# A new issue order for the first part of a one-core trunk layer, with tiles of the modulation moved from VectorE to TensorE

## The chip, the core and the metric

The kernel runs on one core of one Trainium2 chip. The metric is the device time of one execution in microseconds, from a median over runs; lower is better. The core has a matrix engine (TensorE, PE in the profile), a vector engine (VectorE, DVE), an activation engine (ScalarE, ACT), a general engine (GpSimd, POOL) and a queue engine that issues most of the DMAs (SyncE, SP). Each engine works through its own instructions in order and waits on semaphores for the others.

## What is computed

One layer of a diffusion trunk on 1024 tokens of width 1024. Cut to what matters here (the pooling mixer is the one that layer 0 uses):

```
mod_x = silu(c) @ mod_w + mod_b                  # 1024 -> 6 * 1024
sh1, sc1, g1, sh2, sc2, g2 = split(mod_x, 6)
hx  = x * (1 + sc1) + sh1
ox  = multiscale_pool(hx, pool_w, pool_scale)    # 4 groups of 256 channels, windows 2, 4, 8, 16
x   = layer_norm(ALPHA * x + g1 * ox, ln_g[0], ln_b[0])
h   = x * (1 + sc2) + sh2
gt, up = split(h @ ffn_w_in, 2)                  # 1024 -> 2 * 2816
x   = layer_norm(ALPHA * x + g2 * ((silu(gt) * up) @ ffn_w_out), ln_g[1], ln_b[1])
```

Inputs and outputs are float32. `mod_w` alone is 24 MB: each of its six parts (`SH1`, `SC1`, `G1`, `SH2`, `SC2`, `G2`) comes as eight tiles of 128 x 1024.

## The kernel before

Tokens lie in two halves of four blocks of 128 rows: `ORDER = ((1, 2, 3, 4), (5, 6, 7, 0))`. A matrix product in float32 is made of three passes of a rounded format (`mm3`): each operand is split into a high part (`take_hi`, ScalarE) and the rest (`take_lo`, VectorE), and TensorE adds high x high, high x low and low x high.

The kernel has three parts. The **first part** holds the modulation, the pooling, the first norm and the gate product of half 0. Each step of it is a job with a name and a number, and the table `ORDER_OF_ISSUE` lists all jobs in the order in which they are issued. The table therefore sets the order on every engine at once. A second table, `PLACE_OF`, says which PSUM bank (eight of them) and which SBUF buffer (45 large ones) each tile takes; a tile waits until the tile before it in that place has been read for the last time. The **second part** runs 22 periods (`period`) of the products of the feed-forward layer for both halves, with banks `ps_v`. The **third part** makes the output product (`sub_pass`, banks `ps_x` and `ps_y`) and the second norm. The second and the third part are issued by loops that the change doesn't touch.

Jobs of the first part that matter below, by engine:

- SP: `mod_load` (one tile of `mod_w`, named `mw_j_k` for part j and tile k; part 1 is `SC1`, 2 `G1`, 3 `SH2`, 4 `SC2`, 0 `SH1`), `load_x`, `mod_start` (loads a bias row into an accumulator that GpSimd has cleared), `gate_load`, `gate_out`, `keep_row`.
- TensorE: `pool_inner` and `pool_outer` (the window means of a column tile `ct` of half 0 or 1, into bank `ps_pt`), `pooled` (12 matmuls, bank `ps_ox`: the pool weights on four tiles of the means), `mod_col` (8 matmuls, bank `ps_col`: turns a summed modulation row into columns), `mod_whole` (8 matmuls: the same straight from one tile of `mod_w` and the column of silu(c)), `g1_bank`, `turned` (four transposes of x, bank `ps_h`), `gate_step` (6 matmuls of the gate product, bank `ps_gate`; 88 steps, two to eight of each pair of columns at a time).
- VectorE: `mod_add` (adds one tile of `mod_w`, scaled, to the accumulator), `pool_lo`, `make_g1`, `pool_w_weigh`, `pool_w_lo`, `residual` (empties a bank `ps_ox` into x), `mean`, `factor`, `mod_col_done`, `finish_gain`, `finish_shift`, `gate_lo`, `hidden_lo`, and for half 1 `difference` and `t_lo`.
- ScalarE: `pool_hi`, `pool_w_hi`, `start_band`, `end_band`, `spread`, `norm`, `scaled_h` (empties `ps_h` with gain and shift), `hidden_hi`, `gate_hi`, `gate_first`, `gate_done`, `t_hi`.

`mod_columns(j, by_tensor)` shares out the eight tiles of one part: tiles in `by_tensor` become `mod_whole`, the others `mod_add`, and a last `mod_col` adds the accumulator into the same bank. For `SH2` the kernel before gives tiles 0 and 1 to TensorE, for `SC2` none:

```
order = [k for k in range(KT) if k not in by_tensor]
for k in range(KT):
    if k in by_tensor:
        job(mod_whole, j, k, k == by_tensor[0], k == by_tensor[-1] and not order)
    else:
        job(mod_add, j, k, k == order[0])
if order:
    job(mod_col, j, not by_tensor)
```

The last chain before the gate product: all `mod_add` of `SC2` and `SH2`, `mod_col` of both, `finish_gain`, `finish_shift`; and beside it `pooled` and `residual` of half 0, `mean`, `spread`, `factor`, `norm`; then `turned`, `scaled_h`, `hidden_hi`, `hidden_lo`, and `gate_step.0`.

Of the kernel before, what the change touches and what calls it, by code (L numbers as in the profile page):

```python
# [48 lines left out]
mod_load.11 mod_add.4 mod_load.12 mod_load.13 mod_load.14 pool_inner.11 pool_inner.3 mod_load.15 pool_inner.15
pool_inner.7 load_pool_w.0 load_pool_w.1 mod_add.5 load_x.4 pool_outer.2 load_x.5 pool_outer.0 pool_hi.2 pool_outer.3  # L50
pool_outer.1 load_x.6 pool_hi.0 pool_inner.24 pool_lo.2 pool_inner.16 load_x.7 pool_inner.25 pool_hi.3 pool_inner.17
mod_load.16 mod_add.6 pool_inner.28 pool_hi.1 pool_inner.20 mod_load.17 pool_inner.26 pool_inner.18 pool_inner.29
mod_load.18 pool_lo.0 pool_inner.21 start_band.0 scale_bank.0 mod_add.7 mod_load.19 end_band.0 scale_bank.1
scale_row.0 mod_add.8 mod_load.20 mod_col.0 scale_row.1 mod_add.9 mod_load.21 pool_inner.27 pool_outer.6
mod_col_done.0 pool_lo.3 pool_inner.19 pool_outer.4 pool_hi.6 pool_inner.30 mod_add.10 mod_load.22 pool_hi.4
pool_inner.22 pool_inner.31 pool_outer.7 pool_inner.23 pool_outer.5 pool_hi.7 mod_add.11 mod_load.23 pool_hi.5
mod_add.12 mod_load.24 mod_add.13 mod_load.25 mod_add.14 mod_load.26 mod_add.15 mod_load.27 g1_bank.0 pool_lo.1
pool_lo.6 pool_lo.4 g1_bank.1 pool_lo.7 pool_lo.5 make_g1.0 make_g1.1 pool_inner.40 pool_inner.32 pool_w_weigh.0
pool_inner.44 pool_w_weigh.1 pool_inner.36 pool_inner.41 pool_w_weigh.2 pool_inner.33 pool_w_weigh.3 pool_inner.56
pool_inner.48 pool_w_weigh.4 pool_inner.45 pool_w_hi.0 pool_inner.37 pool_w_weigh.5 pool_inner.42 pool_w_weigh.6  # L60
pool_inner.34 pool_inner.57 pool_w_lo.0 pool_inner.49 pool_inner.46 pool_inner.38 pool_inner.43 pool_outer.10 pooled.0
pool_w_weigh.7 pool_hi.10 mod_add.16 mod_load.28 pool_w_hi.1 pooled.2 residual.0 mod_add.17 mod_load.29 pooled.4
mod_add.18 mod_load.30 pool_inner.35 pool_outer.8 pool_inner.47 pool_hi.8 pool_outer.11 residual.2 pool_inner.39
pool_outer.9 pool_hi.11 pool_inner.59 mod_add.19 mod_load.31 gate_load.0 gate_load.1 gate_load.2 gate_load.3
gate_load.4 gate_load.5 pooled.6 pool_hi.9 mod_add.20 pool_outer.14 pool_inner.51 pool_outer.12 pool_inner.58
mod_add.21 pool_inner.50 pool_hi.14 pool_hi.12 residual.4 residual.6 pool_inner.60 mod_add.22 pool_inner.61
pool_inner.52 pool_inner.53 mod_add.23 pool_inner.63 pool_outer.15 pool_inner.55 pool_w_lo.1 pool_outer.13
pool_inner.62 pool_inner.54 pool_lo.10 pool_hi.15 mod_add.24 pool_hi.13 mod_whole.0 pool_lo.8 mod_add.25 mod_whole.1
mod_add.26 pooled.1 mod_add.27 residual.1 pooled.3 mod_add.28 mod_add.29 residual.3 mod_col.2 gate_hi.0 mean.0
spread.0 mean.1 gate_lo.0 pooled.5 spread.1 pool_lo.11 pooled.7 factor.0 residual.5 factor.1 norm.0 mod_col.1 mean.2  # L70
residual.7 keep_row.0 spread.2 mean.3 pool_lo.9 spread.3 pool_lo.14 pooled.12 factor.2 finish_gain.0 finish_shift.0
pooled.14 factor.3 norm.1 pool_lo.12 keep_row.1 norm.2 pool_lo.15 pooled.8 norm.3 pool_lo.13 keep_row.2 pooled.13
residual.12 keep_row.3 gate_hi.2 residual.14 turned.0 gate_hi.1 turned.1 residual.13 gate_lo.2 turned.2 scaled_h.0
turned.3 turned.4 scaled_h.1 gate_lo.1 turned.5 hidden_hi.0 turned.6 turned.7 pooled.15 residual.8 scaled_h.2
scaled_h.3 hidden_lo.0 hidden_hi.1 pooled.10 residual.15 scaled_h.4 hidden_lo.1 gate_step.0 scaled_h.5 hidden_hi.2
gate_step.1 residual.10 scaled_h.6 hidden_lo.2 scaled_h.7 gate_step.2 hidden_hi.3 gate_step.3 gate_hi.4 hidden_lo.3
gate_hi.3 gate_step.4 gate_lo.4 gate_hi.5 gate_lo.3 gate_step.5 gate_lo.5 gate_step.6 mod_load.32 gate_first.0
gate_step.7 mod_load.36 mod_add.30 gate_out.0 gate_first.1 gate_step.8 mod_load.33 gate_out.1 gate_step.9 mod_load.34
gate_step.10 mod_load.35 gate_step.11 gate_load.6 gate_load.7 gate_step.12 mod_add.31 gate_done.0 gate_out.2
gate_step.13 gate_step.14 mod_add.32 gate_step.15 load_pool_w.2 load_pool_w.3 mod_add.33 gate_first.2 gate_step.16  # L80
mod_load.37 mod_add.34 gate_out.3 gate_hi.6 gate_step.17 mod_load.38 gate_lo.6 gate_hi.7 gate_step.18 mod_load.39
gate_lo.7 gate_step.19 gate_load.8 gate_load.9 gate_step.20 gate_done.1 gate_out.4 gate_step.21 gate_step.22
mod_add.35 gate_step.23 gate_first.3 gate_step.24 gate_out.5 gate_step.25 mod_add.36 gate_step.26 mod_add.37
# [1325 lines left out]
```

## Time and profile before

| | |
|---|---|
| median of 3 runs | 749.86 us (748.98 to 750.0) |
| the profiled execution, its own time | 749.97 us |
| its span, first to last instruction | 748.2 us |
| PE busy | 723.9 us (97%) |
| DVE, ACT, POOL busy | 554.9, 274.1, 168.3 us |
| mean granted TensorE clock | 0.967 of full |

The span is cut into stretches by time. PE busy is the time in which at least one matmul is under way; the granted clock says how fast those matmuls ran (1.00 is 2.4 GHz, 0.50 is 1.2 GHz). A stretch in which PE is busy all the time at 1.00 can't get shorter by a change of order; a stretch with idle time or at 0.50 can. The gate product begins at 95.28 us and PE reaches the periods some 130 us later.

### The profile page before, as it was taken

How to read it: one execution, taken by the hardware profiler on the slowest of the kernel's cores; microseconds unless marked ns; L12 is line 12 of the kernel's file. 1: busy time of each engine (PE TensorE's matmuls, PEld its weight loads, DVE VectorE, ACT ScalarE, POOL GpSimd, SP SyncE). 2: the span in 40 equal slices, each digit the busy share in tenths (PEclk: the TensorE clock that was granted, in tenths of full speed). 3: DMA queues.
4: the chain of work that ended last, by engine and by line, in shares of the span. 5: the costliest groups of instructions: out<-in, count | busy, mean ns of one | idle time of the engine just before them, and what ended most of it. 6: DMA issues, size and time to landing. Idle time of an engine off the chain costs nothing.

```text
span 748.2 us, 9131 instructions
## 1 busy us (share of the span) xinstructions
PE 723.9 (97%) x3326; PEld 604.8 (81%) x3326; DVE 554.9 (74%) x675; ACT 274.1 (37%) x353; POOL 168.3 (22%) x133
## 2 busy tenths in 40 slices
PE   6988999999999999999999999999999999999994
PEld 6768988888887888888888888888888888888783
DVE  3797855517288788899998777965878679646986
ACT  0321873435983221311312212212556334336411
POOL 0000000011206546483743624600000000233100
PEclk7587999999999999999999999999999999999998
DMA  8998249674929679797987798455799856999612
GB/s 303 368 409 298 114 159 375 225 237 164 330 86 292 200 239 254 210 310 241 320 264 186 240 265 212 156 202 207 277 376 391 290 193 220 262 302 286 173 57 84
DMA packets 115346, 182.85 MB, mean 244 GB/s; under 512 B 7739, under 2 KB 66819, under 8 KB 115046
## 3 DMA queue, kind: packets, MB, share of 16 engines
q1 hardware_dynamic: 108038, 164.97, 63.8%
q0 software_dynamic: 7264, 17.30, 11.5%
q8 instruction: 26, 0.43, 0.2%
q14 instruction: 18, 0.15, 0.1%
HBM read 142.14 MB, written 51.64 MB: 259 GB/s over the span
## 4 chain that ended last, share of the span: by engine, by line
PE 84%; DVE 7%; DMA 3%; ACT 3%; issue 2%; POOL 0%; SPq 0%; POOLq 0%; DVEq 0%; ACTq 0%
PE ps_v L895 39%; PE ps_x L1106 16%; PE ps_gate L761 14%; PE ps_y L1106 8%; PE ps_col L506 2%; DVE acc L491 2%; DVE ylo L270 1%; PE ps_ox L262 1%; PE ps_ox L263 1%; PE ps_ox L264 1%; DMA x<-in_x 1%; DMA consts<-in_consts 1%; ACT h L699 1%; DMA mw<-in_mod_w 1%; DVE t L270 1%
## 5 line engine op out<-in xcount | busy, mean ns | idle before, releaser
L895 PE MATMUL ps_v<-t,w0h 128*128 128x512 f32 x352 | 109.2, 391 | 0.0
L761 PE MATMUL ps_gate<-h,wih 128*128 128x512 f32 x352 | 109.0, 391 | 0.0
L267 ACT CAST yhi<-yraw 128x1024 fp32r<-128x1024 f32 x77 | 78.4, 1051 | 81.7 <-DMA yraw<-in_ffn_w_out 23.4
L270 DVE TENSOR_TENSOR ylo<-yraw,yhi 128x1024 fp32r<-128x1024 f32 x77 | 91.6, 1218 | 20.6 <-ACT yhi L267 11.4
L962 POOL TENSOR_TENSOR s<-raw,raw 128x512 f32<-128x512 f32 x22 | 31.5, 1432 | 319.3 <-DMA raw<-in_ffn_w_in 300.5
L918 ACT ACTIVATE a<-a 128x512 f32<-128x512 f32 x22 | 13.9, 632 | 229.9 <-DVE a L917 229.9
L895 PEld LDWEIGHTS ps_v<-t,w0h 128*128 128x128 f32 x352 | 66.1, 188 | 14.6 <-issue 1.0
L761 PEld LDWEIGHTS ps_gate<-h,wih 128*128 128x128 f32 x352 | 65.7, 188 | 13.7 <-issue 0.5
L491 DVE SCALAR_TENSOR_TENSOR acc<-mw,s_col,acc 128x1024 f32<-128x1024 f32 x42 | 55.9, 1331 | 19.1 <-DMA mw<-in_mod_w 18.3
L895 PE MATMUL ps_v<-t,w0l 128*128 128x512 f32 x176 | 68.6, 390 | 1.4 <-DVE w0l L270 1.4
L761 PE MATMUL ps_gate<-h,wil 128*128 128x512 f32 x176 | 68.5, 389 | 0.0
L1106 PE MATMUL ps_x<-yhi 128*128 128x512 f32 x176 | 68.5, 389 | 0.0
L1106 PE MATMUL ps_x<-ylo,yhi 128*128 128x512 f32 x176 | 68.5, 389 | 0.0
L1106 PE MATMUL ps_x<-yhi,ylo 128*128 128x512 f32 x176 | 68.5, 389 | 0.0
L895 PE MATMUL ps_v<-t,ws 128*128 128x512 f32 x264 | 63.4, 389 | 0.0
L1068 POOL DMA_DIRECT2D yraw<-in_ffn_w_out x22 | 18.7, 853 | 195.6 <-PE ps_x L1106 163.6
L895 PEld LDWEIGHTS ps_v<-t,ws 128*128 128x128 f32 x264 | 49.5, 188 | 10.3
L895 PE MATMUL ps_v<-h,w1h 128*128 128x512 f32 x176 | 54.2, 389 | 0.0
L895 PE MATMUL ps_v<-t,w1h 128*128 128x512 f32 x176 | 54.2, 389 | 0.0
L1106 PE MATMUL ps_y<-yhi 128*128 128x512 f32 x132 | 51.4, 390 | 0.9 <-DVE yv L1352 0.9
L1106 PE MATMUL ps_y<-yhi,ylo 128*128 128x512 f32 x132 | 51.4, 389 | 0.0
L1106 PE MATMUL ps_y<-ylo,yhi 128*128 128x512 f32 x132 | 51.4, 389 | 0.0
(157 smaller groups left out, 1386.5 us busy)
## 6 DMA issues: line engine op xcount, KB each, us to landing
mw<-in_mod_w SPq DMA_DIRECT2D x48, 512.0 KB, 9.2
raw<-in_ffn_w_in SPq DMA_DIRECT2D x88, 256.0 KB, 5.2
wi<-in_ffn_w_in SPq DMA_DIRECT2D x22, 512.0 KB, 6.2
yraw<-in_ffn_w_out SPq DMA_DIRECT2D x44, 256.0 KB, 5.4
yraw<-ed SPq DMA_DIRECT2D x33, 256.0 KB, 6.0
ed<-in_ffn_w_out POOLq DMA_DIRECT2D x6, 1024.0 KB, 10.5
pd<-pk SPq DMA_DIRECT2D x11, 512.0 KB, 5.2
gd<-gk SPq DMA_DIRECT2D x11, 512.0 KB, 2.9
```

Of the source, the lines that this page charges most:

```text
L262: nc.tensor.matmul(ps, lh, rh, start=first, stop=False)
L263: nc.tensor.matmul(ps, lh, rl, start=False, stop=False)
L267: nc.scalar.copy(hi, src)
L270: nc.vector.tensor_tensor(lo, src, hi.bitcast(F32), ALU.subtract)
L491: nc.vector.scalar_tensor_tensor(acc, w, s_col[:, k : k + 1], acc, ALU.mult, ALU.add)
L506: nc.tensor.matmul(tiles["ps_col", j][:, n * WIDE : (n + 1) * WIDE], t[:, n * P : (n + 1) * P], by, start=first and n == 0, stop=last and ...
L761: nc.tensor.matmul(ps, x, y, start=k == n == 0, stop=k % 4 == 3 and n == 2, skip_group_check=k > 3)
L895: nc.tensor.matmul(ps, x, y, start=fresh and first, stop=last, skip_group_check=not fresh)
L918: nc.scalar.activation(a[:, 1], a[:, 1], ACT.Silu)
L962: nc.gpsimd.tensor_tensor(s, up1, up2, ALU.add)
L1068: nc.gpsimd.dma_start(raw[n][:, 1], ADDED[n // PAIRS](n % PAIRS), accum_op=ALU.add)
L1106: nc.tensor.matmul(ps, s[x][:, r * P : (r + 1) * P], t[y][:, d], start=fresh and j == m == 0, stop=j == PAIRS - 1 and m == 2, skip_group_c ...
```

## The change

The change writes the table `ORDER_OF_ISSUE` anew, with the table of places that belongs to it, and changes which tiles of the second modulation go to TensorE: tile 0 of `SC2` (before: none), and tiles 0 and 7 of `SH2` (before: 0 and 1). No job is added or taken away but for these: `mod_whole` three times in place of two, `mod_add` 37 times in place of 38. The second and third part, all shapes and all arithmetic stay.

```
-BY_TENSOR = (0, 1)
+BY_TENSOR = (0, 7)
...
-vector_rows.0 fill_constants.0 fill_ones.0 mod_load.0 mod_start.0 warm_up.0 load_consts.0 mod_load.1 load_x.0
+vector_rows.0 fill_constants.0 fill_ones.0 mod_start.0 warm_up.0 mod_load.0 load_consts.0 mod_load.1 load_x.0
...
-ps_warm ps_pt0_4 ps_pt1_1 ps_ox1_3_0 ps_h0_5 ps_gate2_0 ps_gate5_1 ps_ox1_1_1 ps_gate9_0
+ps_warm ps_pt0_6 ps_pt1_2 ps_pt1_5 ps_ox1_2_1 ps_gate3_1 ps_h1_4 ps_h1_1 ps_gate7_1
...
-    mod_columns(SC2, ())
+    mod_columns(SC2, (0,))
```

In the table of banks six of the eight `pooled` results of half 0 now share one bank, one after the other: `ps_ox0_0_0 ps_ox0_0_1 ps_ox0_3_0 ps_ox0_2_0 ps_ox0_1_0 ps_ox0_1_1`. On SP the first `mod_start` now stands ahead of the first `mod_load`. The order of all other loads up to the gate weights is as it was. On PE `mod_col` of `SH1` and the two `shift_bank` that follow from it now stand after gate steps 24 and 27, where they stood after steps 26 and 56, and the eight `turned` of half 1 after steps 39 to 41, where they stood after step 71. Four `pooled` of half 1 follow gate step 8, where two followed step 56.

VectorE, `G1` of the modulation (part 2, `acc2`) and the columns of `SC1` (`sc1`). Before, from the last tile of `SC1` on:

```order
L491 SCALAR_TENSOR_TENSOR acc1_192<-mw_1_7_229,s_col_71,acc1_192 128x1024
L491 SCALAR_TENSOR_TENSOR acc2_158<-mw_2_0_233,s_col_71,acc2_158 128x1024
L491 SCALAR_TENSOR_TENSOR acc2_158<-mw_2_1_236,s_col_71,acc2_158 128x1024
L518 SCALAR_TENSOR_TENSOR sc1_73<-ps_col1_323,cols_67 128x8
L474 TENSOR_TENSOR pt0_11_279<-ps_pt0_3_210,pt0_01_269 128x512
L491 SCALAR_TENSOR_TENSOR acc2_158<-mw_2_2_239,s_col_71,acc2_158 128x1024
L491 SCALAR_TENSOR_TENSOR acc2_158<-mw_2_3_243,s_col_71,acc2_158 128x1024
```

The same place in the changed kernel:

```order
L490 SCALAR_TENSOR_TENSOR acc1_188<-mw_1_7_228,s_col_71,acc1_188 128x1024
L490 SCALAR_TENSOR_TENSOR acc2_156<-mw_2_0_233,s_col_71,acc2_156 128x1024
L473 TENSOR_TENSOR pt0_12_332<-ps_pt0_4_301,pt0_02_330 128x512
L490 SCALAR_TENSOR_TENSOR acc2_156<-mw_2_1_236,s_col_71,acc2_156 128x1024
L490 SCALAR_TENSOR_TENSOR acc2_156<-mw_2_2_239,s_col_71,acc2_156 128x1024
L490 SCALAR_TENSOR_TENSOR acc2_156<-mw_2_3_242,s_col_71,acc2_156 128x1024
L490 SCALAR_TENSOR_TENSOR acc2_156<-mw_2_4_246,s_col_71,acc2_156 128x1024
L490 SCALAR_TENSOR_TENSOR acc2_156<-mw_2_5_248,s_col_71,acc2_156 128x1024
L490 SCALAR_TENSOR_TENSOR acc2_156<-mw_2_6_250,s_col_71,acc2_156 128x1024
L490 SCALAR_TENSOR_TENSOR acc2_156<-mw_2_7_254,s_col_71,acc2_156 128x1024
L473 TENSOR_TENSOR pt0_12_332<-ps_pt0_5_351,pt0_02_330 128x512
L517 SCALAR_TENSOR_TENSOR sc1_73<-ps_col1_321,cols_67 128x8
```

The step that reads the columns of `SC1` from TensorE's bank (`sc1`) stood among the adds of `G1` and now stands behind all of them.

TensorE, where two tiles of `SH2` (`mw_3_*`) go through `mod_whole` into bank `ps_col3`. Before, with the last window means of half 1 (`ps_pt1`) ahead and `pooled` of half 0 behind:

```order
L461 MATMUL ps_pt1_7_533<-starts_306,x0_283 128x128
L466 MATMUL ps_pt1_7_533<-consts_72,halo_207 128x2x8
L461 MATMUL ps_pt1_5_537<-starts_306,x0_283 128x128
L466 MATMUL ps_pt1_5_537<-consts_72,halo_207 128x2x8
L461 MATMUL ps_pt1_7_533<-ends_314,x7_273 128x135
L461 MATMUL ps_pt1_5_537<-ends_314,x7_273 128x131
L506 MATMUL ps_col3_555<-s_col_71,mw_3_0_361 128x64 x8
L506 MATMUL ps_col3_555<-s_col_71,mw_3_1_364 128x64 x8
```

The same two in the changed kernel, behind the last `pooled` of half 0 (`ps_ox0_3_1`), with window means of half 1, the `mod_col` of `SH2` and the first transpose behind:

```order
L263 MATMUL ps_ox0_3_1_611<-wpsh1_421,pt0_13_378 128x256
L505 MATMUL ps_col3_630<-s_col_71,mw_3_0_349 128x64 x8
L505 MATMUL ps_col3_630<-s_col_71,mw_3_7_480 128x64 x8
L460 MATMUL ps_pt1_4_657<-consts_72,x5_263 128x132
L460 MATMUL ps_pt1_4_657<-consts_72,x6_269 128x135
L460 MATMUL ps_pt1_4_657<-starts_266,x0_280 128x128
L465 MATMUL ps_pt1_4_657<-consts_72,halo_207 128x2x8
L460 MATMUL ps_pt1_4_657<-ends_276,x7_273 128x131
L505 MATMUL ps_col3_630<-ones_69,acc3_555 128x64 x8
L460 MATMUL ps_pt1_5_689<-consts_72,x5_263 128x132
L460 MATMUL ps_pt1_5_689<-consts_72,x6_269 128x135
L693 MATMUL ps_h0_2_692<-ident_68,x1_177 128x128
```

`mod_whole` of `SH2` moved from the middle of the window means and `pooled` of half 0 to behind all `pooled` of half 0, directly ahead of the transposes.

VectorE, at the end of the gate product, where the split weights of the second part begin (`w1l`, `ws1`, `w0l` of block 0, 1). Before:

```order
L270 TENSOR_TENSOR w1l_0_1890<-raw0_1_1337,w1h_0_1888 128x1024
L854 TENSOR_TENSOR h32_1_3_1716<-h32_1_3_1716,h32_0_1_831 128x1024
L270 TENSOR_TENSOR ws1_1_1905<-s1_1883,ws1_1_1905 128x512
L854 TENSOR_TENSOR h32_0_3_877<-h32_0_3_877,h32_1_3_1716 128x1024
L270 TENSOR_TENSOR t2_11_1867<-h32_1_3_1716,t2_01_1863 128x1024
L270 TENSOR_TENSOR t4_11_1869<-h32_0_3_877,t4_01_1865 128x1024
L270 TENSOR_TENSOR w0l_1_1910<-raw1_0_1553,w0h_1_1908 128x1024
```

The same place in the changed kernel:

```order
L269 TENSOR_TENSOR wil10_0_1763<-wi_10_0_1718,wih10_0_1740 128x1024
L269 TENSOR_TENSOR wil10_1_1774<-wi_10_1_1720,wih10_1_1765 128x1024
L269 TENSOR_TENSOR w1l_0_1897<-raw0_1_1485,w1h_0_1895 128x1024
L269 TENSOR_TENSOR ws1_1_1912<-s1_1890,ws1_1_1912 128x512
L269 TENSOR_TENSOR w0l_1_1917<-raw1_0_1678,w0h_1_1915 128x1024
```

The differences and splits of half 1 (`h32`, `t2`, `t4`) that stood between the weights of the second part have moved far ahead, into the middle of the gate product.

## Rows read from the trace of the kernel before

**Rows 1.** The page, busy time of TensorE: busy microseconds, share of the span, instructions.

```profile
PE 723.9 (97%) x3326; PEld 604.8 (81%) x3326; DVE 554.9 (74%) x675; ACT 274.1 (37%) x353; POOL 168.3 (22%) x133
```

**Rows 2.** Stretches of the span: from:to and length, then the busy time of PE, PEld, DVE, ACT and POOL (instructions), the granted clock, the DMA share and GB/s.

```profile
20.60:40.20 19.60, 16.75 (x68) 14.14 (x68) 14.94 (x16) 6.81 (x14) 0.00 (x0) 0.59 1.01 379
40.20:61.60 21.40, 21.13 (x132) 17.56 (x132) 20.55 (x33) 5.67 (x9) 0.00 (x0) 0.93 1.03 408
61.60:78.40 16.80, 14.41 (x73) 14.09 (x73) 11.97 (x17) 3.22 (x6) 0.00 (x0) 0.59 0.61 200
78.40:95.30 16.90, 16.90 (x147) 16.90 (x147) 13.63 (x34) 16.73 (x23) 0.00 (x0) 1.00 0.41 152
95.30:225.00 129.70, 129.70 (x607) 107.95 (x606) 67.05 (x93) 78.26 (x108) 10.33 (x8) 1.00 0.65 225
240.00:700.00 460.00, 460.00 (x2027) 380.14 (x2026) 369.26 (x409) 147.75 (x174) 145.43 (x109) 1.00 0.82 255
```

**Rows 3.** Waits of TensorE over the whole span: who was waited for, us in total, times, longest.

```profile
PE ps_g L548 <- DVE acc L491: 2.9, 1, 2.9
PE ps_col L506 <- DVE pt L474: 1.6, 1, 1.6
PE ps_v L895 <- DVE w0l L270: 1.4, 1, 1.4
```

**Rows 4.** TensorE in order of time, before the gate product: start, length, line, what, count, and the idle time ahead of it where there was some. A float32 matmul of the code shows as two, so eight columns of `mod_col` or `mod_whole` are x16.

```profile
40.23 3.51 PE L548 MATMUL ps_g<-acc,ones 128*128 128x512 f32 x4 [2.89 <-DVE acc L491]
43.58 2.41 PE L461 MATMUL ps_pt<-consts,x 128*128 128x130 f32 x20
...
63.23 6.56 PE L506 MATMUL ps_col<-s_col,mw 128*128 128x64 f32 x32 [1.60 <-DVE pt L474]
...
73.25 0.58 PE L262 MATMUL ps_ox<-wpsh,pt 128*128 128x256 f32 x1 [0.79 <-DVE x L608]
...
75.97 2.63 PE L506 MATMUL ps_col<-ones,acc 128*128 128x64 f32 x16
...
81.36 1.90 PE L506 MATMUL ps_col<-ones,acc 128*128 128x64 f32 x16
...
88.91 3.65 PE L694 MATMUL ps_h<-ident,x 128*128 128x128 f32 x32
92.33 0.36 PE L262 MATMUL ps_ox<-wpsh,pt 128*128 128x256 f32 x1
...
95.28 0.63 PE L761 MATMUL ps_gate<-h,wih 128*128 128x512 f32 x2
...
95.98 0.62 PE L761 MATMUL ps_gate<-h,wih 128*128 128x512 f32 x2
```

**Rows 5.** VectorE in order of time over the same stretch, columns as in rows 4.

```profile
31.53 0.17 DVE L518 SCALAR_TENSOR_TENSOR sc<-ps_col,cols 128x8 f32<-128x8 f32 x1 [3.01 <-PE ps_col L506]
...
32.21 7.88 DVE L491 SCALAR_TENSOR_TENSOR acc<-mw,s_col,acc 128x1024 f32<-128x1024 f32 x6
40.01 3.07 DVE L474 TENSOR_TENSOR pt<-ps_pt,pt 128x512 fp32r<-128x512 f32 x5
...
44.39 2.85 DVE L570 SCALAR_TENSOR_TENSOR wp<-wp,sc,g 128x256 f32<-128x256 f32 x7
...
48.70 0.75 DVE L489 TENSOR_SCALAR acc<-mw,s_col 128x1024 f32<-128x1024 f32 x1
...
61.36 1.22 DVE L270 TENSOR_TENSOR wpsl<-wp,wpsh 128x1024 fp32r<-128x1024 f32 x1
...
72.50 0.69 DVE L608 SCALAR_TENSOR_TENSOR x<-x,ps_ox 128x512 f32<-128x512 f32 x1 [4.22 <-PE ps_ox L264]
...
73.11 2.60 DVE L491 SCALAR_TENSOR_TENSOR acc<-mw,s_col,acc 128x1024 f32<-128x1024 f32 x2
```

**Rows 6.** ScalarE in order of time, the norms and the hidden tiles of half 0.

```profile
85.40 3.50 ACT L645 ACTIVATE x<-x,mv 128x1024 f32<-128x1024 f32 x3
...
90.68 1.44 ACT L699 ACTIVATE h<-ps_h,shift,gain 128x512 f32<-128x512 f32 x2
92.16 1.05 ACT L267 CAST h<-h 128x1024 fp32r<-128x1024 f32 x1
```

**Rows 7.** ScalarE, then VectorE, in order of time where the second part begins.

```profile
231.79 0.62 ACT L267 CAST ws<-s 128x512 fp32r<-128x512 f32 x1 [3.02 <-POOL s L962]
232.32 1.05 ACT L267 CAST t<-h 128x1024 fp32r<-128x1024 f32 x1
...
233.40 2.18 DVE L270 TENSOR_TENSOR t<-h,t 128x1024 fp32r<-128x1024 f32 x1 [2.88 <-ACT t L267]
235.50 2.30 DVE L270 TENSOR_TENSOR w0l<-raw,w0h 128x1024 fp32r<-128x1024 f32 x1
```

**Rows 8.** SP's queue at the start: start and length of the issue of a DMA.

```profile
1.20 0.36 SPq L295 DMA_DIRECT2D mw<-in_mod_w  x1
2.27 0.25 SPq L383 DMA_DIRECT2D acc<-in_mod_b  x1
```

**Rows 9.** SP, VectorE and TensorE around the last tile of `SH1`, in the gate product.

```profile
118.31 0.86 SPq L295 DMA_DIRECT2D mw<-in_mod_w  x2
...
127.48 2.61 DVE L491 SCALAR_TENSOR_TENSOR acc<-mw,s_col,acc 128x1024 f32<-128x1024 f32 x2 [1.22 <-DMA mw<-in_mod_w]
...
133.39 1.89 PE L506 MATMUL ps_col<-ones,acc 128*128 128x64 f32 x16
```

More of the change, by code (lines that the diff above doesn't have):

```diff
@@ L49 @@
[L49 to L83, printed above, removed]
@@ new lines @@
+mod_whole.0 mod_load.28 pool_w_lo.1 pooled.0 mod_add.16 mod_load.29 mod_add.17 mod_load.30 pool_outer.8 pool_inner.63
+pool_outer.15 pool_inner.61 residual.0 pool_inner.43 pool_outer.10 pool_inner.34 pooled.1 mod_add.18 mod_load.31
+gate_load.0 gate_load.1 gate_load.2 gate_load.3 gate_load.4 gate_load.5 pool_hi.10 pool_hi.8 mod_add.19 pool_inner.47
+pool_outer.11 pool_inner.38 pool_hi.11 pool_inner.62 pool_inner.58 residual.1 pool_hi.9 mean.0 pooled.6 mod_add.20
+pool_hi.14 spread.0 mod_add.21 residual.6 mod_add.22 pooled.4 pool_hi.15 factor.0 mod_col.1 mod_add.23 norm.0
@@ new lines @@
+residual.4 keep_row.0 mod_add.24 pooled.2 finish_gain.0 pooled.5 residual.2 mod_add.25 pooled.3 residual.5 residual.3
+pooled.7 mean.2 mean.1 spread.2 mod_add.26 mod_whole.1 residual.7 spread.1 mean.3 factor.2 mod_whole.2 mod_add.27
+norm.2 mod_add.28 pool_inner.48 spread.3 keep_row.2 pool_inner.49 pool_inner.51 pool_outer.12 pool_inner.50 factor.1
+mod_col.2 pool_lo.10 norm.1 factor.3 pool_lo.11 norm.3 keep_row.1 pool_lo.14 pool_inner.52 pool_inner.53 turned.2
+gate_hi.0 finish_shift.0 keep_row.3 turned.4 pool_lo.8 turned.3 scaled_h.2 pool_lo.9 turned.1 scaled_h.4 gate_lo.0
@@ new lines @@
+gate_step.7 mod_load.36 pool_lo.12 gate_out.0 gate_first.1 pool_lo.13 gate_step.8 mod_load.33 mod_add.29 gate_out.1
+pooled.11 pooled.9 residual.11 mean.5 spread.5 pooled.15 residual.9 mean.4 mod_add.30 spread.4 pooled.13 residual.15
+gate_step.9 mod_load.34 factor.4 residual.13 norm.4 mod_add.31 gate_step.10 mod_load.35 keep_row.4 factor.5
+gate_step.11 gate_load.6 mod_add.32 gate_load.7 norm.5 gate_done.0 gate_step.12 keep_row.5 mod_add.33 gate_step.13
+gate_out.2 gate_step.14 gate_hi.6 gate_step.15 load_pool_w.2 load_pool_w.3 gate_lo.6 gate_hi.7 gate_step.16
@@ L180 @@
+pt0_10 pt1_10 h0_13
+mw_4_3 pt1_03 wi_4_0 wih6_1 t4_01
+mw_4_4 sq1 sq3 h0_01
+pt0_02 h32_0_3 wil9_1
+pt0_12 h0_00
+mw_4_5 acc3 wih1_1 wil5_0 pk6 t2_10
+mw_4_6 sq2 wih2_0 acc_v h32_1_0 w0h_0
+mw_4_7 sq4 wil2_0 wi_5_1 wi_7_1 wil8_0 wih9_1
 """,
```

171 lines of the change are left out of this document (91 added, 80 removed).

## The prediction

> **What bounds the kernel now.** First the busy times: TensorE has work under way 97% of the span [rows 1]. Then the stretches: from 78.4 us to 225 and from 240 to 700 TensorE is busy in every microsecond at clock 1.00 [rows 2]; there only fewer matmuls could help, and the change adds eight. What can be won lies ahead of 78.4, where the granted clock is 0.59 in two of three stretches and TensorE idles 2.9 us between 20.6 and 40.2 and 2.4 us between 61.6 and 78.4, and in one wait of 1.4 us after 225 [rows 2, 3]. So I ask two things of the new order: how early does the gate product begin, and how much TensorE work has been pushed behind its begin? Every microsecond that it begins earlier counts, less that pushed work, because TensorE is full from there on.
>
> The begin hangs on a chain through VectorE. The adds of the modulation run nearly without a gap from 32 us; the last one ends at 75.7, then come `mod_col`, the norms on ScalarE until 88.9, the transposes at 88.9 and the gate product at 95.28 [rows 4 to 6]. In that chain VectorE waits 3.01 us for the columns of `SC1` and 4.22 us for a `pooled` that stands behind two `mod_whole` on TensorE; those two take 6.56 us, 0.205 us an instruction, against 1.90/16 = 0.119 at the later `mod_col` [rows 4, 5].
>
> **Part 1: the loads start later.** `mod_start` ahead of the first `mod_load` makes that load wait until GpSimd has cleared the accumulator: it is issued after 2.27 + 0.25 us and not at 1.20 [rows 8]. The first tile loses 1.3 us, the others one issue of 0.4 us. Where the first adds wait for loads, all that follows is late by 0.4 to 1.3 us; I take 0.7, nearer the lower end, since only one tile is late by the whole.
>
> **Part 2: the sum of `G1`.** The wait of 3.01 us goes, because the read of the columns now stands behind all adds of `G1`. Two more `pool_lo` stand ahead of the last add (five, before three), at 3.07/5 = 0.61 us [rows 5]. The last add ended at 32.21 + 7.88 = 40.1; now at 40.1 - 3.0 + 1.2 + 0.7 = 39.0. What is late next is TensorE, whose window means of half 0 end at about 37 at the lower clock, so it waits for the sum as before.
>
> **Part 3: the pool weights.** From 39.0: three `pool_lo` 1.8, two `make_g1` 1.5 (from 43.0 to 44.4), eight `pool_w_weigh` at 2.85/7 = 0.41 make 3.3, both `pool_w_lo` at 1.15 make 2.3: VectorE is free at 47.9. Before, the first add of `SC2` began at 48.70 with the second `pool_w_lo` still to come at 61.36 [rows 5].
>
> **Part 4: the adds of `SC2` and `SH2`.** Thirteen on VectorE (before fourteen): eleven at 1.3 and two first ones at 0.75 make 15.8. Between them stand all eight `residual` of half 0 at 0.68, 5.4 us, and some 1.5 us of `mean`, `factor` and `finish_gain`; the three splits that stood there before now stand behind or ahead. Tile 7 of `SH2`, the last to land, needs no add any more. Without a wait the last add ends at 47.9 + 22.7 = 70.6. With waits it is later: six `pooled` share one bank, so each waits for the `residual` of the one before, and that for VectorE. A `pooled` takes (95.28 - 92.33)/2 = 1.48 us at the full clock [rows 4]; I let TensorE and VectorE take turns step by step and find 1.6 us of wait for VectorE in all and one of 1.4 us for TensorE (it waits for the `residual` that is queued behind two adds). Bounds: 0 and, with `pooled` at the lower clock (from 73.25 to 75.97, 2.7 us), 5. The last add then ends at 72.2, 3.5 us earlier than before. The third `mod_whole` costs TensorE 8 columns, 1.9 us at the full clock and 3.3 at the lower [rows 4]; it lies at about 48, ahead of the first `pooled`, and is inside that walk.
>
> **Part 5: to the gate product.** TensorE ends the `pooled` of half 0 near 67.5, the two `mod_whole` near 71.2, window means of half 1 (0.24 us each by 2.41/10) near 72.5, and `mod_col` of `SH2` near 74.3. ScalarE ends the last norm at 74.9: only `norm` of two rows is left behind the adds, against three in a row from 85.4 to 88.9 before [rows 6]. The transposes begin at 75 and not at 88.9. They take 3.65, four `pooled` 5.9 and the last window means 0.9: 85.4. Beside them ScalarE needs 1.05 for a weight, eight `scaled_h` at 0.72, 1.05 for `hidden_hi`, and VectorE 1.2: 84, so TensorE sets the end [rows 4, 6]. With 0.6 for hand-overs the gate product begins at 86.0, 9.3 us earlier.
>
> **Part 6: behind it.** Four `pooled` follow that begin and before only two did: +3.0. In the gate product the `mod_col` of `SH1` has moved from behind step 26 to behind step 24, and `shift_bank` from step 56 to step 27. TensorE works in order, so both hold up all gate steps behind them. A step is six matmuls, 2 x 0.70 = 1.4 us [rows 4], so `mod_col` comes up about 40 us after the begin, with the four `pooled` in between. The last tile of `SH1` is issued behind the store of pair 2, about 31 us after the begin (16 steps, four `pooled`, and the casts that ScalarE does ahead of that store). Before, a tile issued at 118.31 was added from 127.48 on, 9.2 us later [rows 9]; with that and an add of 1.3 the sum is ready at 41.5, 1.5 us late, and with a faster landing it is in time. I take 0.8 of 0 to 1.6. At the end of the gate product the wait of 1.4 us goes: VectorE split `t4` behind a ScalarE cast that stood behind `ws` of the block after, which waited for GpSimd, and only then the `w0l` that TensorE wanted [rows 3, 7]. The changed order does that split half a gate product earlier. Before 700 and behind, nothing moves.
>
> **Sum**, against the profiled execution of 749.97 (0.11 above the median of 749.86, so no correction): -9.3 + 3.0 + 0.8 - 1.4 = -6.9: **743.1 us**.
>
> **Rivals.** The sum holds the clock at 2.4 GHz from about 43 us, where it rose before (stretch 40.2:61.6: 0.93). This is the weak place.
>
> *The clock falls at the pair of `mod_whole`.* For it: from 63.23 on TensorE ran 6.56 us of nothing else without a gap, at the pace of 1.2 GHz, and the stretch has 0.59. Against it: the wait of 1.60 us came first, and the `mod_col` at 81.36 lies in a stretch of 1.00 [rows 2, 4]. The pair then costs 6.6 in place of 3.8, the means 2.8 for 1.4, `mod_col` 2.6 for 1.9: 4.9 less 0.7 of slack ahead of the transposes, 747.3. The Trainium skill says in TensorE: Matmul & The Clock Gate, "What's actually happening", that the gate sets the rate by how busy the engine has been recently. By that rule alone a pair without a gap would keep the clock, and the time would be 743.1; the trace agrees only in part, since those 6.56 us, busy throughout, did not raise it.
>
> *The loads of `SH1` don't move with the gate product.* Their last add ended at 130.1 [rows 9]. If the store queue ahead of them holds them there, TensorE waits at `mod_col` from 125.8: 4.3 in place of 0.8, 746.6. So the change would not do all that an early gate product promises.
>
> *Slower: the clock falls at the single bank.* TensorE waits for a `residual`, runs the `mod_col` of `SC2` (1.9 us), and waits again for the one bank. If the clock falls there, near 58 us, and stays down up to the transposes, four `pooled` cost 1.25 more each, two `mod_col` 1.5, `mod_whole` 2.8, window means 1.9 and the transposes 3.65 (twice as long): 14.8 less 2.1 of slack, 755.8. It decides from 8.4 us on, so if the fall lasts from the four `pooled` through `mod_whole` at least. For it: the 16.8 us stretch of 0.59 began with a wait of just that size. Against: that fall was over by 78.4, with `pooled` and a `mod_col` running.
>
> **How the numbers follow.** About 0.2%, 1.5 us, can be told from no change. The forecast and its neighbourhood (741 to 745.5) get 0.42; the lower edge, with loads late by 0.4 only and none of the waits of parts 4 and 6 (743.1 - 0.3 - 1.6 - 0.8 = 740.4), 0.05; the clock at `mod_whole` 0.20; the loads of `SH1` 0.13; two of these together, near 749 to 751, 0.08; slower 0.12. Faster is the sum of the first four, 0.80; same 0.08; slower 0.12. The range 740.5 to 749.5 leaves out the lower edge, half of the pairs and the slower case, about 0.2.
>
> **What would show it.** Right: the first gate matmul near 86; the last add of `SH2` near 72; no row of VectorE waiting for `ps_col`; no wait of `ps_v` for `w0l`; a wait at `mod_col` of `SH1` under 2 us; 1.00 in the stretches from 45 to 86. Wrong: a stretch of 0.50 between 58 and 80, a first gate matmul behind 92, or a new wait of TensorE inside the gate product of more than 4 us.

## The result and the profile after

The changed kernel took 745.85 us in the median of six runs (743.82 to 746.52), the kernel before 749.75 in the same series; the ratio is 0.9943, 95% interval [0.9925, 0.9962]. Two later series with the same kernel gave 0.9917 [0.9895, 0.9939] and 0.9918 [0.9894, 0.9941]. The series did not all run on one chip, so from here on ratios are compared, or times of one series.

The profiled execution took 743.82 us, the shortest of the six; the others ran 0.8 to 2.7 us longer at mean granted clocks of 0.970 to 0.973 against its 0.974, and no profile shows where they lose it. Its span is 742.0. Its stretches, in the columns of [rows 2]:

```profile
20.60:40.20 19.60, 18.75 (x63) 14.02 (x61) 16.06 (x16) 5.94 (x12) 0.00 (x0) 0.50 1.01 368
40.20:61.60 21.40, 20.08 (x129) 17.26 (x129) 19.52 (x31) 8.34 (x13) 0.00 (x0) 0.91 1.03 409
61.60:78.40 16.80, 16.80 (x145) 16.58 (x145) 15.34 (x38) 10.50 (x16) 0.00 (x0) 1.00 0.92 320
78.40:95.30 16.90, 16.90 (x112) 15.22 (x111) 13.50 (x17) 15.05 (x20) 0.00 (x0) 1.00 0.28 101
95.30:225.00 129.70, 129.70 (x617) 108.46 (x616) 73.41 (x98) 73.96 (x102) 14.99 (x8) 1.00 0.67 227
240.00:700.00 460.00, 460.00 (x2027) 380.18 (x2026) 370.12 (x408) 150.17 (x176) 144.48 (x107) 1.00 0.82 253
```

The stretch from 61.6 to 78.4, which had 2.4 us of idle time at 0.59, is now full at 1.00. The one ahead of 40.2 is fuller than before, and slower: 0.50 throughout. TensorE's waits, all of 0.8 us or more:

```profile
PE ps_pt L460 <- DMA x<-in_x: 5.6, 4, 4.2
PE ps_ox L261 <- DVE x L607: 1.3, 1, 1.3
PE ps_warm L320 <- DVE ones L310: 1.1, 1, 1.1
PE ps_y L1105 <- DVE yv L1351: 0.9, 1, 0.9
PE ps_pt L465 <- DMA consts<-in_consts: 0.8, 1, 0.8
```

The three waits of [rows 3] (for the sum of `G1`, ahead of `mod_whole`, for `w0l`) are gone. The wait for a `residual`, 0.79 us in [rows 4], is now one of 1.32. TensorE in order of time (start, length), for [rows 4]:

```profile
30.65 3.67 PE L505 MATMUL ps_col<-ones,acc 128*128 128x64 f32 x16
...
42.39 2.81 PE L547 MATMUL ps_g<-acc,ones 128*128 128x512 f32 x4
...
49.67 1.90 PE L505 MATMUL ps_col<-s_col,mw 128*128 128x64 f32 x16
...
61.09 0.39 PE L261 MATMUL ps_ox<-wpsh,pt 128*128 128x256 f32 x1 [1.32 <-DVE x L607]
...
70.18 3.68 PE L505 MATMUL ps_col<-s_col,mw 128*128 128x64 f32 x32
...
75.17 1.89 PE L505 MATMUL ps_col<-ones,acc 128*128 128x64 f32 x16
...
77.41 1.96 PE L693 MATMUL ps_h<-ident,x 128*128 128x128 f32 x16
...
87.83 0.73 PE L760 MATMUL ps_gate<-h,wih 128*128 128x512 f32 x2
...
127.74 1.89 PE L505 MATMUL ps_col<-ones,acc 128*128 128x64 f32 x16
```

The pair of `mod_whole` takes 3.68 us and not 6.56, the transposes come at 77.4 and not at 88.9, the gate product begins at 87.83 and not at 95.28. VectorE, for [rows 5] and [rows 9], and at the end SP's issue of the last tile of `SH1`:

```profile
31.37 0.69 DVE L473 TENSOR_TENSOR pt<-ps_pt,pt 128x512 fp32r<-128x512 f32 x1 [1.55 <-ACT pt L470]
31.98 9.20 DVE L490 SCALAR_TENSOR_TENSOR acc<-mw,s_col,acc 128x1024 f32<-128x1024 f32 x7
...
51.34 0.75 DVE L488 TENSOR_SCALAR acc<-mw,s_col 128x1024 f32<-128x1024 f32 x1
...
72.12 2.60 DVE L490 SCALAR_TENSOR_TENSOR acc<-mw,s_col,acc 128x1024 f32<-128x1024 f32 x2
...
125.62 1.28 DVE L490 SCALAR_TENSOR_TENSOR acc<-mw,s_col,acc 128x1024 f32<-128x1024 f32 x1 [1.19 <-DMA mw<-in_mod_w]
...
117.54 0.49 SPq L294 DMA_DIRECT2D mw<-in_mod_w  x1
```

The last add of `G1` ends at 41.18, the first of `SC2` begins at 51.34, the last of `SH2` ends at 74.72. The last add of `SH1` ends at 126.90, 0.84 us before TensorE comes to its `mod_col` at 127.74.

**The account.** The gate product begins 7.45 us earlier; four `pooled` follow its begin in place of two, 2.95; the wait of 1.41 is gone: 749.97 - 7.45 + 2.95 - 1.41 = 744.06, against 743.82 measured. So all of the difference but 0.24 us is made ahead of the gate product and at the head of the second part, as the prediction had it.

### The profile page after: what moved, and what is told of

It reads as the page before. It is cut to its first block, busy times and chain, and to the rows that moved or that the text cites. A ratio compares the mean times of both kernels' runs of the same rounds, so it can differ in the third digit from the quotient of the medians.

```text
span 742.0 us, 9155 instructions
## 1 busy us (share of the span) xinstructions
PE 722.5 (97%) x3342; PEld 602.2 (81%) x3342; DVE 555.0 (75%) x674; ACT 273.7 (37%) x353; POOL 174.1 (23%) x133
## 4 chain that ended last, share of the span: by engine, by line
PE 91%; DVE 4%; DMA 2%; ACT 1%; issue 0%; POOL 0%; SPq 0%; POOLq 0%; DVEq 0%; ACTq 0%
PE ps_v L894 40%; PE ps_gate L760 16%; PE ps_x L1105 16%; PE ps_y L1105 8%; PE ps_pt L460 2%; PE ps_col L505 2%; DVE ylo L269 1%; PE ps_ox L261 1%; PE ps_ox L263 1%; PE ps_ox L262 1%; PE ps_h L693 1%; DMA x<-in_x 1%; PE ps_pt L465 1%; DMA mw<-in_mod_w 1%; DMA consts<-in_consts 1%; ACT scratch L1153 1%
## 5 line engine op out<-in xcount | busy, mean ns | idle before, releaser
L961 POOL TENSOR_TENSOR s<-raw,raw 128x512 f32<-128x512 f32 x22 | 35.0, 1593 | 309.2 <-DVE t L269 167.1
```

The source lines that it names most:

```text
L961: nc.gpsimd.tensor_tensor(s, up1, up2, ALU.add)
```

## The experiments

Theory: the new order gives the gain, through an earlier gate product, and the tiles on TensorE give little. Rivals: the tiles carry it, or a lucky phase of the clock does. Two parts of the change were taken for losses or gains of their own (late loads, the split at the end of the gate product) and are tried too.

**The changed kernel again**, twice, as the yardstick.

> The changed kernel once more, as the yardstick for the others of this series. Its profiled execution took 743.8 us, while the other five took 744.6 to 746.5, with mean granted clocks of 0.970 to 0.973 against 0.974. Theory: the order leaves the clock ahead of 80 us near an edge, so the time comes out between 743.8 and 746.5 with a median near 745.8, and a profile that takes about 2 us longer shows a stretch below 1.00 between 45 and 80 us (where the profiled one of 743.8 has none). Rival: the spread has nothing to do with the clock in the first part; then a profile near 746 shows 1.00 from 45 us on and its first gate matmul still at 87.8.

Measured: 744.42 (743.46 to 746.06), ratio 0.9917 [0.9895, 0.9939]. The profiled run, 743.46, began the gate product at 86.67, 1.16 us earlier than the run above. `G1` on TensorE began 0.34 us earlier (42.05), and the rest is the clock, which rose earlier. Kernel, slice, its length, PE busy, granted clock, DMA share, GB/s; first the run of 743.82, then this one:

```profile
40.00:42.00 2.00, 2.00 (x9) 0.50 1.03 410
42.00:44.00 2.00, 2.00 (x4) 0.50 1.03 410
44.00:46.00 2.00, 2.00 (x12) 0.98 1.03 410
```

```profile
40.00:42.00 2.00, 2.00 (x9) 0.61 1.02 405
42.00:44.00 2.00, 2.00 (x8) 1.00 1.04 414
```

The two banks of `G1` (four matmuls in the profile, taken together as the bank of `G1` from here on) took 1.98 us here and 2.81 there. So the rise of the clock, at about 41.6 us here and 44.1 there, moves the gate product by most of a microsecond. Not all of that arrives: 0.36 of the 1.16 us were left at the end, and 0.3 of the rest went into a wait of `shift_bank` for VectorE that the run above didn't have. The question of the expectation, where a run of 746 us loses its time, stays open, since no such run was profiled.

> The changed kernel again, beside the one with the extra matmuls. Expected at 744 to 746; the clock's last rise ahead of the gate product at 41 to 45 us, the first gate matmul at 86.7 to 88.

Measured: 743.04 (742.21 to 745.78), ratio 0.9918 [0.9894, 0.9941]; gate product at 86.3, the rise at about 43.3. The time and the gate product lie a little under what was expected. The rise came later than in the first repeat and the gate product earlier, because the bank of `G1` began at 40.16 already: the first tiles had come only 0.3 to 0.5 us later than in the kernel before (1.1 to 1.2 in the run of 743.82), and the clock was 1.00 from about 19.4 to 22.8 us, where that run shows 0.50.

One thing stays the same in all three. From the first matmul behind the bank of `G1` to the first gate matmul it is 42.8 us: 45.04 to 87.83, 43.87 to 86.67, 43.53 to 86.33. The same 42.8 us lie between them in four of the edited kernels below, and 43.1 to 43.6 in the other four, where the clock was still 0.50 behind the bank or fell later on. So with the clock up again, what moves the gate product lies ahead of the end of that bank.

**The order without the tiles, and the tiles without the order.**

```
-BY_TENSOR = (0, 7)
+BY_TENSOR = (0, 1)
-    mod_columns(SC2, (0,))
+    mod_columns(SC2, ())
```

In the table one more `mod_add` stands in place of the first `mod_whole`.

> The new order without the new tiles: all eight tiles of SC2 go to VectorE, and TensorE takes tiles 0 and 1 of SH2 as before. Theory: the order carries the gain. VectorE has one add more, 1.3 us, and TensorE one mod_whole less, 1.9 us, ahead of the first pooled result, where TensorE was the later one; so the gate product begins between 0.5 us earlier and 1.3 us later than in the changed kernel, and the time lies at 744 to 746. Rival: the tiles on TensorE carry 2 us or more; then the time is 746.5 or above and the gate product begins 2 us later.

Measured: 745.70 (744.90 to 746.57), ratio 0.9940 [0.9918, 0.9962], gate product at 88.05. The theory holds: the order alone gives 0.6%. The changed kernel has 0.9943 and twice 0.992, so within the new order the tiles are worth nothing to 0.25%, with intervals that overlap. Where they help can be seen. Without the `mod_whole` at 49 us TensorE waits 1.16 us at the second `pooled`, and the clock falls there (columns as for the slices above):

```profile
54.41 0.41 PE L261 MATMUL ps_ox<-wpsh,pt 128*128 128x256 f32 x1 [1.16 <-ACT pt L470]
```

```profile
52.00:54.00 2.00, 1.25 (x8) 1.00 1.01 395
54.00:56.00 2.00, 1.59 (x8) 0.64 1.04 416
56.00:58.00 2.00, 2.00 (x10) 0.51 1.02 406
58.00:60.00 2.00, 2.00 (x17) 1.00 1.03 401
```

The fall lasts some 3.4 us, so it costs about 1.7 us of work at the full clock; with the wait of 1.16 that is more than the 1.9 us of the `mod_whole` that is saved. From the first matmul behind the bank of `G1` to the gate product it is 43.5 us here in place of 42.8. It is an event like that of the slower rival, at another wait and over before it could spread to the transposes.

The other half, edited into the kernel before:

```
-BY_TENSOR = (0, 1)
+BY_TENSOR = (0, 7)
-    mod_columns(SC2, ())
+    mod_columns(SC2, (0,))
+... pooled.7 factor.0 residual.5 factor.1 norm.0 mod_whole.0 mod_col.1 mean.2 ...
```

> The kernel before with the new tiles alone: tile 0 of SC2 straight ahead of the mod_col of SC2 on TensorE, and tiles 0 and 7 of SH2 there in place of 0 and 1; the order of before otherwise. Theory: no gain. In the order of before VectorE waits 4.22 us at a pooled result that stands behind two mod_whole, so an add saved ahead of that lengthens the wait, and mod_whole in front of mod_col lies in idle time of TensorE; the time is that of the kernel before within 1 us, the first gate matmul at 95 to 96. Rival: the saved add of 1.3 us comes through to the gate product, first gate matmul at 94.0 and 1.3 us less.

Measured: 751.56 against 751.05 before, ratio 1.0016 [0.9999, 1.0033]: no gain, and the gate product came at 96.78, a little later than expected. VectorE, then TensorE's waits from 60 to 100 us:

```profile
50.66 0.69 DVE L608 SCALAR_TENSOR_TENSOR x<-x,ps_ox 128x512 f32<-128x512 f32 x1 [1.77 <-PE ps_ox L264]
...
73.04 0.69 DVE L608 SCALAR_TENSOR_TENSOR x<-x,ps_ox 128x512 f32<-128x512 f32 x1 [4.69 <-PE ps_ox L264]
```

```profile
PE ps_col L506 <- DVE pt L474: 1.4, 1, 1.4
PE ps_col L506 <- DMA mw<-in_mod_w: 1.4, 1, 1.4
PE ps_col L506 <- DVE acc L491: 0.8, 1, 0.8
```

The saved add stood ahead of the first `residual`. VectorE waits 1.77 us there now, where it waited 0.61 in the kernel before:

```profile
50.05 0.69 DVE L608 SCALAR_TENSOR_TENSOR x<-x,ps_ox 128x512 f32<-128x512 f32 x1 [0.61 <-PE ps_ox L264]
```

So it comes to the second wait at 73.04 - 4.69 = 68.35 us, and came there at 72.50 - 4.22 = 68.28 before [rows 5]: nothing of the add is left. A part of the longer first wait may be the clock, which rose at about 45.8 us in this profile and at 43.4 before. The second wait is longer because its `pooled` comes later: TensorE now waits 1.4 us ahead of it for the last tile of `SH2` to land. The fall of the clock was shorter here (0.80 in the stretch 61.6:78.4, 0.59 before), and the gate product came no earlier for it.

**The columns read early again**, the wait that part 2 of the prediction removes.

```
-... mod_add.8 mod_load.20 mod_col.0 pool_hi.4 pool_lo.4 mod_add.9 ... pool_lo.5 g1_bank.0 mod_col_done.0 pool_lo.6
+... mod_add.8 mod_load.20 mod_col.0 pool_hi.4 pool_lo.4 mod_col_done.0 mod_add.9 ... pool_lo.5 g1_bank.0 pool_lo.6
```

> The read of the columns of SC1 stands ahead of the first two thirds of the adds of G1 again (ahead of the add that began at 31.98 in the changed kernel); all else as changed. Theory: TensorE finishes those columns at 34.32, so VectorE waits 2.3 us there; the last add of G1 ends at 43.6 in place of 41.2, and since TensorE itself was ready for the first bank of G1 only at 42.4, the time rises by 1.2 us. Rival, the prediction's own step, which had TensorE ready at 37: the whole wait counts, 2.4 us. Third: nothing, if later waits (the one bank of the pooled results) take it up.

Measured: 747.14 (746.07 to 747.59), 2.7 us above the changed kernel of the same series (744.42); the gate product came at 90.14, 3.5 us later than in the first repeat. VectorE, TensorE, and the clock behind it:

```profile
33.58 0.17 DVE L517 SCALAR_TENSOR_TENSOR sc<-ps_col,cols 128x8 f32<-128x8 f32 x1 [2.30 <-PE ps_col L505]
```

```profile
43.02 3.75 PE L547 MATMUL ps_g<-acc,ones 128*128 128x512 f32 x4 [1.34 <-DVE acc L490]
```

```profile
44.00:48.00 4.00, 4.00 (x11) 0.50 1.03 410
48.00:50.00 2.00, 2.00 (x19) 0.97 1.02 406
```

The wait is 2.30 us, as both sides expected, and the cost that of the rival (2.4). But the way to it is another: TensorE was ready at 41.7 in this run, not at 37, so the wait made the bank of `G1` only 1.0 us later than in the first repeat; the rest came with the clock, which stayed at 0.50 up to 48.1 us and made the bank take 3.75 us for 1.98. What of that second part is due to the wait and what to chance, this run can't tell.

**The first load early again.**

```
-... fill_ones.0 mod_start.0 warm_up.0 mod_load.0 load_consts.0 ...
+... fill_ones.0 mod_load.0 mod_start.0 warm_up.0 load_consts.0 ...
```

> The first load of the modulation stands ahead of the start of the accumulator again, as in the kernel before; all else as changed. Theory: the late loads (VectorE's first waits for tiles end 1.1 to 1.2 us later than before, TensorE's wait for the constants 1.1 later) delay the whole chain up to the gate product, since TensorE is busy without a gap from 21.7 to 44 at 0.50 and the loads run one after the other: the first bank of G1 begins at 41.3 in place of 42.4 and the first gate matmul at 86.7 in place of 87.8, the time is 1.1 us under that of the changed kernel of this series. Rival: the shift is taken up by waits later on (the one bank of the pooled results, loads of SC2), first gate matmul at 87.8 and no difference.

Measured: 744.11 (741.48 to 745.06), ratio 0.9902 [0.9880, 0.9924] beside 0.9917 for the changed kernel of the series: no difference that can be told. The bank of `G1` began at 41.58, 0.81 us earlier than in the run of 743.82, but at 0.50 up to about 44.6, so the gate product came at 87.70; the expected 86.7 would have needed the earlier rise. The 0.81 can't be put down to the load: without any edit that bank began at 42.39, 42.05 and 40.16.

**The last split late again.**

```
-... t_hi.7 t_lo.6 gate_step.63 ... gate_first.8 t_lo.7 gate_step.64 ...
+... t_lo.6 gate_step.63 ... gate_first.8 gate_step.64 ... gate_out.21 t_hi.7 t_lo.7
-pt0_02 h32_0_3 wil9_1
+pt0_02 h32_0_3
-mw_4_3 pt1_03 wi_4_0 wih6_1 t4_01
+mw_4_3 pt1_03 wi_4_0 wih6_1 wil9_1 t4_01
```

> Only the cast and the rest of the last split term of half 1 (t_hi and t_lo number 7, t4) stand at the end of the table again; one gate weight (wil9_1) and the place of t4 change so that nothing else has to wait for it; all else as changed. Theory of the prediction: VectorE comes to the w0l that TensorE wants only after that split, so the wait at the first ps_v comes back, 1.4 us as before, and the time rises by 1.4 us against the changed kernel. Rival: the wait of before came from the row of casts and differences around that split, which stands earlier now; then no wait of ps_v for w0l over 0.3 us and no difference in time.

Measured: 743.85 (740.78 to 745.12), ratio 0.9908 [0.9878, 0.9937], and no wait at `ps_v`. ScalarE, then VectorE:

```profile
221.32 1.04 ACT L266 CAST t<-h 128x1024 fp32r<-128x1024 f32 x1
...
229.75 0.63 ACT L266 CAST ws<-s 128x512 fp32r<-128x512 f32 x1 [2.38 <-POOL s L961]
```

```profile
222.40 1.23 DVE L269 TENSOR_TENSOR t<-h,t 128x1024 fp32r<-128x1024 f32 x1 [9.13 <-ACT t L266]
```

The rival holds for this edit: a split at 222.4 costs nothing here; its cast stands ahead of `ws` (221.32 against 229.75) and not behind it as in [rows 7]. So the experiment doesn't rebuild the queue of before. That the wait belongs to the old order is shown all the same: it is there in all three profiles of that order (1.4, 1.5 and 1.7 us) and in none of the eleven of the new one. Which of the splits and casts brings it about stays open. The trace of before points at `t4`, which stands directly ahead of `w0l` on VectorE and waits there for its cast [rows 7], but no run confirms it. With the last two differences, casts and splits all moved back and every place as it is, the jobs wait for each other in a circle, so that order has no time; it was not tried with other places.

**Work for TensorE in the early waits.** These kernels add matmuls of ones by ones into the bank of `warm_up`, which nothing reads.

```
+MORE = (9, 3, 3, 3, 5)
+    def more_warm(n):
+        for _ in range(n):
+            nc.tensor.matmul(tiles["warm",][:, :P], ones, ones, start=True, stop=True)
-... vector_rows.1 to_columns.0 vector_rows.2 ...
+... vector_rows.1 to_columns.0 more_warm.0 vector_rows.2 ...
```

The other four, `more_warm.1` to `more_warm.4`, stand behind the four groups of x in the same way.

> The changed kernel with 23 more matmuls of ones by ones (nothing reads them) in TensorE's idle time up to 21.7 us: nine behind the first columns, three behind each of the next three groups of x, five behind the fourth. In the runs so far the clock was 1.00 for a few us near 18 to 21 in three of four, fell at 21 to 22 beside a wait, and rose for good at 41.3, 44.3, 44.7 and 48 us, while TensorE was busy without a gap from 22 on. Theory: the waits ahead of 22 us are what takes the clock down; filled, it stays at 1.00 from there on, the window means of half 0 end near 33, VectorE's last add of G1 at 41.2 sets the first bank of G1, which takes 2.0 in place of 3.5 us, and the first gate matmul comes at 86.0 to 86.7 in every run: 1 to 1.7 us under the changed kernel's profiled 743.8, and a narrower spread. Rival: the clock falls all the same; then the extra matmuls (0.46 us each at 0.50) make TensorE late by up to 2.7 us at the first bank of G1 and the time rises by 1 to 3 us.

Measured: 741.59 (740.98 to 743.84), ratio 0.9891 [0.9863, 0.9919], gate product at 84.90. Its clock:

```profile
16.00:22.00 6.00, 4.96 (x41) 1.00 0.96 327
22.00:28.00 6.00, 6.00 (x22) 0.56 0.99 345
28.00:34.00 6.00, 6.00 (x22) 0.50 1.02 413
34.00:40.00 6.00, 6.00 (x22) 0.52 1.06 381
40.00:42.00 2.00, 2.00 (x7) 1.00 1.01 401
```

The ratio is lower than the three of the changed kernel, though it overlaps with two of their intervals, and the theory is wrong: the clock fell at about 22.7 us, when TensorE had been at work without a gap since 21.1. In this profile a part of the early work ran at 1.00, and the rise came at about 39.8, ahead of the bank of `G1` at 40.3.

> Both edits that helped or could help: the first load of the modulation ahead of the start of the accumulator, and the 23 extra matmuls up to 21.7 us. With the extra matmuls alone the first bank of G1 began at 40.3 straight behind VectorE's adds, the clock being 1.00 by then, and the gate product at 84.9 (profiled time 740.98, median 741.59). Theory: with TensorE no longer the later engine there, VectorE is, and it gets its tiles 1.1 us earlier by the early load; so the first bank of G1 begins near 39.2 and the gate product near 83.8, and the median is 1.1 us lower, 740.5. Rival: the clock rises later than the bank (it rose at 39.5 in that run); then the bank and what follows run at 0.50 up to the rise and nothing is won, 741.6.

Measured: 743.10 (741.09 to 745.09), ratio 0.9928 [0.9905, 0.9952]: nothing won, the rival. The bank of `G1` began at 38.17, 2.1 us earlier, but the clock rose only at 42.5, the bank took 3.75 us, and the gate product came at 84.9 again. At its end the weights of the last pair were late: ScalarE waited 6.97 us for one to land, up to 198.85, and TensorE 0.84 for VectorE's half of it, up to 202.93.

> Of the 23 extra matmuls only the nine behind the first columns (6.5 to about 10.5 us). Theory: these nine, over the longest wait (4.2 us in the changed kernel), keep the clock up; then the stretch from 16 to 23 is at 1.00 and the rise comes at 39 to 40, as with all 23, time 741.6. Rival: the fills between the groups of x do it; then the clock is as in the changed kernel, rises at 41 to 45, and the time is 744.4.

Measured: 744.89 (743.39 to 746.22), ratio 0.9948 [0.9928, 0.9969], the rival: nine fills alone do nothing, the clock rose at about 47 us in the profiled run.

> The kernel before, order and tiles untouched, with the same 23 extra matmuls at the same places (behind the columns and the groups of x). Theory: what the extra matmuls give is a matter of the clock and has nothing to do with the order; but here VectorE's sum of G1 ends at 40.1 with TensorE idle ahead of it for 2.9 us, so only what follows can gain: the bank of G1 at 1.00 takes 2.0 in place of 3.5 us, the first gate matmul comes up to 1.5 us earlier than 95.28, and the time lies 0 to 1.5 us under the kernel before. Rival: in the old order too the fall at 62 to 78 us depends on the early part; then the time drops by 3 us or more and part of the gain of the new order was luck with the clock.

Measured: 748.36 (746.95 to 751.95) against 748.96, ratio 0.9995 [0.9978, 1.0011]. In the old order the fills win nothing that can be told. In its profile (748.04) the bank of `G1` began at 38.08 and the gate product at 93.00, 2.3 us earlier than in the kernel before and more than the theory allowed, but the median doesn't follow it. And the fall of the clock between 62 and 78 us stays (0.60 in that stretch, 0.59 before). So the gain of the new order there is no luck with the early clock.

> The changed kernel with the 23 extra matmuls once more, now beside the changed kernel itself on one chip, since the intervals of the two so far overlap. Theory: the fills shorten the low stretch of the clock ahead of the first bank of G1 (16 us in their first run, 20 to 34 without them), and the median is 2 us or more under that of the changed kernel here. Rival: when the clock rises is chance from run to run, as the two runs with fills and the early load, or with the first fill alone, make likely (rise at 42.5 and 46.6); then the medians lie within 1 us.

Measured: 741.79 (740.91 to 742.23), ratio 0.9891 [0.9871, 0.9912], in one series with the changed kernel's 743.04 (742.21 to 745.78). The five runs lie at or under 742.23, the six of the changed kernel at or above 742.21. That is 1.25 us, between theory and rival. The fills alone have the same ratio in both series, 0.2 to 0.3% under that of the changed kernel; the intervals overlap, and the run with the fills and the early load (0.9928) has no such gain. So a gain of that size is likely and not settled. The first matmul behind the bank of `G1` came at 42.3 here and at 42.1 in the first series (43.5 to 45.0 without fills), the gate product at 85.09. The rise came at 42.0 us here and at 39.8 in the first series, so its instant is not what the fills hold fast.

## Why the prediction was right, and where it was not

The forecast was 743.1. The medians of three series lie 3.9, 6.8 and 6.4 us under the kernel before, where the sum had -6.9. The mechanism is the one that the prediction named. That the profiled execution, 743.82, came so near is in part luck: it is the shortest of six with a median of 745.85, and in it two terms were off, one each way, the begin of the gate product by 1.83 us and the wait for `SH1` by 0.8.

**Part 1** can't be told from the spread between runs. The first tiles came 1.1 to 1.2 us later than before in the first profile, 1.2 to 1.4 in the first repeat and 0.3 to 0.5 in the second; 0.7 was taken, of 0.4 to 1.3. What it costs in the end couldn't be told either (0.9902 without it, 0.9917 with it).

**Part 2 failed in one step:** TensorE, "whose window means of half 0 end at about 37 at the lower clock". They ended at 42.4. The 37 was carried over from the trace of before, where the clock was up for a part of the stretch, and not at the lower clock throughout; the same slices of before and of after:

```profile
22.00:28.00 6.00, 6.00 (x26) 0.64 0.99 371
28.00:34.00 6.00, 6.00 (x27) 0.64 1.03 404
```

```profile
22.00:28.00 6.00, 6.00 (x22) 0.50 0.96 325
28.00:34.00 6.00, 6.00 (x24) 0.50 1.03 411
```

12 us at 0.64 do the work of 12 x 0.64/0.50 = 15.4 us at 0.50, 3.4 more; with the late loads of 1.1 that makes 41.5 of the 42.4. It was no chance of one run: from 23 to 39 us the clock is 0.50 in all eight profiles of the new order without fills between the groups of x. What keeps it down there is not shown. The slower means also held up ScalarE and through it VectorE, 1.55 us at 31.37; so the last add of `G1` ended at 41.2 and not at 39.0. That VectorE no longer waits for `SC1`, and that such a wait is dear, is shown (+2.7 us when put back, of which the profile puts 1.0 down to the wait itself).

**Part 3**: 3.4 us late at the first add of `SC2` (51.34 for 47.9): 2.2 from part 2, and waits of 0.67 for ScalarE and 0.57 for the bank of `G1`, which ran at 0.50.

**Part 4** was right: VectorE waited 0.43 + 0.73 + 0.38 = 1.54 us for `pooled` (1.6 forecast), TensorE 1.32 for a `residual` (1.4 forecast), and from the first to the last add it took 23.4 us (24.3 forecast).

**Part 5**: the chain from the last add to the gate product was right, 87.83 - 74.72 = 13.1 us against 86.0 - 72.2 = 13.8. The begin was 1.8 us late, and that came with the bank of `G1`, since from its end on it is 42.8 us in all three profiles of this kernel. In the repeats, where that bank ended earlier, it was 86.67 and 86.3.

**Part 6**: 3.0 and 1.4 were right in size. The wait at `mod_col` of `SH1` was 0 and not 0.8: the last add was ready 0.84 us ahead of TensorE. The last tile was issued 29.7 us after the begin, where 31 was forecast, and added 8.1 us later, where 9.2 was. (In the table of before, `mod_col` of `SH1` stands behind step 27 and the two `shift_bank` behind 55 and 56; the sum doesn't rest on it.) In the repeats there were 0.3 to 0.4 us of waits further on. This is the term that made up for part of the lateness.

**The rivals.** The clock did not fall at the pair of `mod_whole`, nor at the wait of 1.3 us for the single bank: behind its rise it is 1.00 up to 100 us in ten of the eleven profiles of the new order. In the eleventh, the order without the tiles, it fell at the other wait of 1.16 us and was back within 4 us, 1.7 us of work and not the 14.8 less slack of the slower rival. The loads of `SH1` were not held: their last add ended at 126.90, before at 130.1, with four `pooled` now ahead of it, and at 123.66 in the first profile with the 23 extra matmuls, whose gate product began at 84.90. That the change might do nothing is ruled out by the three series. The clock mattered most where the sum had not asked about it, ahead of 45 us.
